# A ring of weight buffers refilled by the half buffer

## The chip, the cores and the metric

The kernel runs on one core of a Trainium2 chip. The metric is the device time of one execution in microseconds (us). It is the median of three runs; a profiled execution beside them gives the trace.

## The reference

One layer of a bidirectional encoder on 512 tokens of width 1024, in float32. Three token mixers (neighbourhood attention, grouped-query attention, attention into 256 memory tokens) are gated and merged, and a layer norm follows. Behind it stands an expert-choice mixture: 16 experts take 64 tokens each.

```python
def expert_choice_ffn(x, w_router, w_gate_up, w_down):
    ...
    gate, idx = lax.top_k(jnp.swapaxes(aff, 1, 2), cap)
    xs = x[bidx, idx]
    h = jnp.einsum('becd,edf->becf', xs, w_gate_up)
    hg, hu = jnp.split(h, 2, axis=-1)
    ye = jnp.einsum('becf,efd->becd', jax.nn.silu(hg) * hu, w_down)
    ye = ye * gate[..., None].astype(ye.dtype)
    return jnp.zeros_like(x).at[bidx, idx].add(ye)
```

The weights of the experts are 16 x (1024 x 2048 + 1024 x 1024) float32 values, 192 MB (of 2^20 bytes). They are read once.

## The kernel before

The program has two stages: the token mixers with the first norm and the routing (up to about 520 us), and the experts with the second norm. Each engine works through its instructions in the order in which they were written. SyncE (SP) issues all transfers of weights, in the order of the program, and an issue that has to wait holds back those behind it.

**Units.** The expert weights are cut into 192 units of 1 MB, [128 partitions x 2048 floats]. A unit `("gu", e, k)` is one of eight parts, along the contraction, of expert e's gate and up matrices; `("dn", e, k)` is one of four parts of its down matrix. `_blocks()` (L44) puts them in the order of use: expert e's first four gate-up units, then the down units of expert e-1, then the rest of expert e's; at the end the gate-up units of expert 15, and the down units of experts 14 and 15.

**The ring.** Twelve places in on-chip memory, listed in `RING` (L32), hold weights in turn; ten have room for two units, `raw` and `VS` for one. The places belong to tiles of the first stage and come free at its end. A *round* is one pass through the list. `ROUNDS` ends the use of `raw` after one round, and of `G1` and `VS` after two. Round one is 12 transfers with 22 units. A *block* is what a place takes in one round: its tag, its width, its units, whether its units are transferred apart (the last `N_SINGLE` units are), and whether the place is used again. In DRAM a block of two units is laid out so that each partition reads 16 KB in one piece.

`Ring.load()` (L807) allocates a new tile at the block's place and issues its transfer at L817, or one per unit at L815 where the units are apart. `Ring.get()` hands out a unit. `Ring.done()` (L835) is called behind the matmuls of a unit, counts down the units that are left in its block, and lends the place on when none is left: the next block is loaded, which waits for the matmuls of both old units.

**The use.** `gate_up(e, ks)` (L1277) does four matmuls for each unit, two for g and two for u (L1285); in the trace each is two instructions, so a unit is 8 records. `down(e)` (L1310) does the same for the down units (L1320), and `last_down` (L1418) for those of expert 15, in quarters of the columns (L1440). While expert 0 runs, steps of a `gather` (L1245, L1247) stand between its units. `combine` adds an expert pair's outputs into the accumulator. In the last expert the residual is prepared ahead, so that behind the last weights little is left: four quarter products, their splits and sums, the statistics of the norm, and eight output transfers (L1547).

Of the kernel before, what the change touches and what calls it, by code (L numbers as in the profile page):

```python
# [18 lines left out]
P = 128  # L19
D = 1024  # L20
# [11 lines left out]
RING = (("Q2", 2), ("Q1", 2), ("Q5", 2), ("Q7", 2), ("Q4", 2), ("Q3", 2), ("Q6", 2), ("raw", 1), ("Q9", 2), ("VS", 1),  # L32
        ("G1", 2), ("M", 2))
ROUNDS = {"raw": 1, "G1": 2, "VS": 2}
N_SINGLE = 10
X_SCALE = 1024.0
A_SCALE = 16384.0

# [1 line left out]
def lead(e):  # L40
    return 2 if e == NEXP - 2 else 4


def _blocks():  # L44
    order = []
    for e in range(NEXP - 1):
        order += [("gu", e, k) for k in range(lead(e))]
        if e:
            order += [("dn", e - 1, k) for k in range(4)]
        order += [("gu", e, k) for k in range(lead(e), KD)]  # L50
    order += [("gu", NEXP - 1, k) for k in range(KD)]
    order += [("dn", e, k) for e in (NEXP - 2, NEXP - 1) for k in range(4)]
    blocks, i, r = [], 0, 0
    while i < len(order):
        for tag, n in RING:
            left = ROUNDS.get(tag, len(order)) - r
            if left > 0 and i < len(order):
                blocks.append((tag, n, order[i:i + n], i + n > len(order) - N_SINGLE, left > 1))
                i += n
        r += 1  # L60
    return blocks

# [2 lines left out]
def layer_kernel(ctx: ExitStack, tc: tile.TileContext, xt, xn, first0, wu, bgate, rpb, gains, wrt,  # L65
                 lnp, lnt, wx, csn, nmask, tri, iota, out, dbg=None):
    nc = tc.nc
# [12 lines left out]
    def R(tag, shape, name, dt=F32, bufs=None):  # L80
        return rp.tile(shape, dt, name=name, tag=tag, bufs=bufs)
# [55 lines left out]
    class Stream:  # L137
        AHEAD_DMA = 2

        def __init__(self):  # L140
            self.nd = 0
            self.ns = 0
            self.used = 0
            self.raw = {}
            self.hl = {}
# [647 lines left out]
    class Ring:  # L793
        def __init__(self):
            self.blocks = _blocks()
            self.at = {}
            self.row = [0]
            for b, (_, n, keys, _, _) in enumerate(self.blocks):
                self.row.append(self.row[-1] + P * n)
                for j, key in enumerate(keys):  # L800
                    self.at[key] = (b, j)
            self.n = 0
            self.left = [len(b[2]) for b in self.blocks]
            self.lent = len(RING)
            self.t = {}
            self.free_at_end = []

        def load(self):
            tag, n, keys, apart, _ = self.blocks[self.n]
            r0 = self.row[self.n]  # L810
            full = R(tag, [P, 2 * n, D], f"w{self.n}")
            src = wx[r0:r0 + P * len(keys)].rearrange("(p j) (h c) -> p (j h) c", j=len(keys), h=2)
            if apart:
                for j in range(len(keys)):
                    nc.sync.dma_start(full[:, 2 * j:2 * j + 2], src[:, 2 * j:2 * j + 2])  # L815
            else:
                nc.sync.dma_start(full[:, :2 * len(keys)], src)  # L817
            for j, key in enumerate(keys):
                t = [full[:, 2 * j + h] for h in range(2)]
                if key[0] == "dn" and key[1] == NEXP - 1:  # L820
                    t = [x.rearrange("p (c n) -> p c n", c=4) for x in t]
                self.t[key] = t
            self.n += 1
# [9 lines left out]
            return self.t.pop(key)  # L833

        def done(self, *key):  # L835
            b, _ = self.at[key]
            self.left[b] -= 1
            if self.left[b] == 0:
                tag, again = self.blocks[b][0], self.blocks[b][4]
                if again:  # L840
                    if self.lent >= len(self.blocks):
                        self.free_at_end.append(tag)
                    self.lent += 1
            self.upto(self.lent)

    ring = Ring()
# [800 lines left out]
def _down_slots(w):  # L1647
    import numpy as np
    a = w.reshape(NEXP, 4, 2, 128, 1024).swapaxes(2, 3).reshape(NEXP, 4, 128, 2048).copy()
    a[-1] = w[-1].reshape(2, 4, 128, 4, 256).transpose(3, 2, 0, 1, 4).reshape(4, 128, 2048)  # L1650
    return a


def _expert_rows(wgu, wdn):
    import numpy as np
    dn = _down_slots(wdn)
    unit = {"gu": lambda e, k: wgu[e, k * P:(k + 1) * P], "dn": lambda e, k: dn[e, k]}
    return np.concatenate([np.stack([unit[t](e, k) for t, e, k in keys], 1).reshape(-1, 2048) for _, _, keys, _, _ in _blocks()])


def _norm_rows(g1, b1, g2, b2):
# [17 lines left out]
def _prep(inp):  # L1679
# [51 lines left out]
    for ty in range(3):  # L1731
# [20 lines left out]
        "lnp": _norm_rows(*(np.asarray(inp[n])[0] for n in ("ln1_g", "ln1_b", "ln2_g", "ln2_b"))),  # L1752
        "lnt": np.stack([np.asarray(inp[n])[0].reshape(8, 128).T for n in ("ln1_g", "ln1_b")], 1),
        "wx": _expert_rows(np.asarray(inp["w_gate_up"])[0], np.asarray(inp["w_down"])[0]),
        "csn": csn, "nmask": nmask, "tri": tri,
        "iota": np.broadcast_to(np.arange(1, 65, dtype=f), (128, 64)),
# [24 lines left out]
```

## Time and profile before

| | |
|---|---|
| runs | 971.08 us median of 3 (971.02 to 971.66) |
| profiled execution, its own time | 973.19 us |
| its span, first to last instruction | 971.3 us |
| granted TensorE clock, mean | 0.996 |
| read from HBM | 247.46 MB |
| DMA queue of SP (q1): packets, MB, share of 16 engines | 37550, 249.74 MB, 63.3% |
| weight transfers | 89 of 2048 KB, 14 of 1024 KB |

The profile gives for each engine the time in which it was busy. PE is the matrix engine, PEld its weight loads, DVE, ACT and POOL are the vector, scalar and GpSimd engines, and SP issues transfers. In the table of stages a row is a stretch of the span: its bounds, its length, then the busy time of each engine with the number of instructions, the granted clock of PE, the mean share of time in which the 16 DMA engines were busy, and the GB/s that they moved. The chain of waits is followed back from the last instruction, at each step to what released it. A matmul that has been issued can count as busy, so a busy PE isn't at its peak by that alone.

### The profile page before, as it was taken

How to read it: one execution, taken by the hardware profiler on the slowest of the kernel's cores; microseconds unless marked ns; L12 is line 12 of the kernel's file. 1: busy time of each engine (PE TensorE's matmuls, PEld its weight loads, DVE VectorE, ACT ScalarE, POOL GpSimd, SP SyncE). 2: the span in 40 equal slices, each digit the busy share in tenths (PEclk: the TensorE clock that was granted, in tenths of full speed). 3: DMA queues.
4: the chain of work that ended last, by engine and by line, in shares of the span. 5: the costliest groups of instructions: out<-in, count | busy, mean ns of one | idle time of the engine just before them, and what ended most of it. 6: DMA issues, size and time to landing. Idle time of an engine off the chain costs nothing.

```text
span 971.3 us, 13273 instructions
## 1 busy us (share of the span) xinstructions
PE 948.8 (98%) x5444; PEld 619.5 (64%) x5444; DVE 454.8 (47%) x866; ACT 276.0 (28%) x544; POOL 79.3 (8%) x86
## 2 busy tenths in 40 slices
PE   9999999999999999999999999999999999998996
PEld 9899878889888888887886333433344333532344
DVE  6347668875376566237464122653322222231426
ACT  5334444544354454323223111100010001100123
POOL 0002303000032231000013000000000000000003
PEclk9999999999999999999999999999999999999998
DMA  9321111211333322575818999999999999999992
GB/s 360 111 68 65 65 66 44 66 46 64 85 112 112 100 82 83 218 285 201 366 61 340 406 431 430 431 430 430 431 431 429 430 431 430 430 429 430 429 396 89
DMA packets 38330, 251.21 MB, mean 259 GB/s; under 512 B 12911, under 2 KB 13295, under 8 KB 24830
## 3 DMA queue, kind: packets, MB, share of 16 engines
q1 hardware_dynamic: 37550, 249.74, 63.3%
q8 instruction: 43, 0.70, 0.3%
q10 hardware_dynamic: 720, 0.62, 0.2%
q14 instruction: 17, 0.14, 0.0%
HBM read 247.46 MB, written 2.10 MB: 257 GB/s over the span
## 4 chain that ended last, share of the span: by engine, by line
PE 80%; DMA 10%; DVE 6%; ACT 1%; issue 1%; POOL 1%; DVEq 0%; POOLq 0%; ACTq 0%; SPq 0%
DMA w<-in_wx 10%; PE g L1285 9%; PE u L1285 9%; PE y L1320 8%; PE gate L274 4%; PE gate L276 4%; PE gate L275 4%; PE pr L274 2%; PE gy L649 2%; PE ga L1245 2%; PE pr L275 2%; PE pr L276 2%; PE nqk L274 1%; PE nqk L275 1%; PE nqk L276 1%; PE gt L636 1%
## 5 line engine op out<-in xcount | busy, mean ns | idle before, releaser
L1285 PE MATMUL g<-w,xs 128*64 128x512 f32 x512 | 135.1, 606 | 3.6 <-DMA w<-in_wx 3.6
L1285 PE MATMUL u<-w,xs 128*64 128x512 f32 x512 | 131.6, 592 | 0.0
L1320 PE MATMUL y<-w,hT 128*64 128x512 f32 x480 | 106.8, 594 | 4.4 <-DMA w<-in_wx 3.7
L93 DVE TENSOR_TENSOR y<-y,y 64x512 fp32r<-64x512 f32 x30 | 20.7, 689 | 134.8 <-ACT y L92 134.8
L1285 PEld LDWEIGHTS u<-w,xs 128*64 128x64 f32 x512 | 36.8, 137 | 73.1 <-issue 72.3
L92 ACT CAST y<-y 64x512 fp32r<-64x512 f32 x30 | 17.4, 579 | 226.1 <-PE y L1320 214.8
L1320 PEld LDWEIGHTS y<-w,hT 128*64 128x64 f32 x480 | 33.7, 137 | 73.8 <-issue 63.2
L93 DVE TENSOR_TENSOR los<-raw_twin,whi 128x1024 fp32r<-128x1024 f32 x43 | 54.1, 1258 | 52.5 <-ACT whi L92 52.3
L276 PE MATMUL gate<-xh,los 128*128 128x512 f32 x192 | 74.8, 390 | 0.0
L1285 PEld LDWEIGHTS g<-w,xs 128*64 128x64 f32 x512 | 30.6, 136 | 55.0 <-issue 43.3
L274 PE MATMUL gate<-xh,whi 128*128 128x512 f32 x160 | 63.5, 397 | 0.0
L275 PE MATMUL gate<-xl,whi 128*128 128x512 f32 x160 | 62.3, 390 | 0.0
L1392 DVE TENSOR_TENSOR acc<-acc,cb 128x512 f32<-128x512 f32 x56 | 35.6, 684 | 37.7 <-PE cb L1390 37.7
L92 ACT CAST whi<-raw_twin 128x1024 fp32r<-128x1024 f32 x43 | 45.1, 1049 | 8.3 <-PE wo L1085 4.4
L93 DVE TENSOR_TENSOR los<-raw_twin,los 128x1024 fp32r<-128x1024 f32 x21 | 26.5, 1260 | 35.5 <-ACT los L92 35.4
L1461 POOL TENSOR_TENSOR acc<-acc,ln2g 128x512 f32<-128x512 f32 x6 | 7.6, 1276 | 432.7 <-DVE l2s L1489 430.7
L276 PEld LDWEIGHTS gate<-xh,los 128*128 128x128 f32 x192 | 36.0, 188 | 7.7
L625 ACT ACTIVATE att_twin<-gs,nm 128x512 f32<-128x512 f32 x32 | 21.7, 683 | 52.4 <-DVE nm L624 52.4
L1295 ACT ACTIVATE tg<-g 128x512 f32<-128x512 f32 x16 | 9.5, 597 | 90.2 <-PE g L1285 90.2
L274 PEld LDWEIGHTS gate<-xh,whi 128*128 128x128 f32 x160 | 30.0, 188 | 7.1 <-issue 1.2
L275 PEld LDWEIGHTS gate<-xl,whi 128*128 128x128 f32 x160 | 30.1, 188 | 5.9
L1308 DVE COPY hT<-ht 128x512 f32<-128x512 f32 x15 | 10.4, 691 | 44.4 <-PE ht L1303 44.4
(420 smaller groups left out, 1902.4 us busy)
## 6 DMA issues: line engine op xcount, KB each, us to landing
w<-in_wx SPq DMA_DIRECT2D x89, 2048.0 KB
raw_twin<-in_wu SPq DMA_DIRECT2D x65, 512.0 KB
w<-in_wx SPq DMA_DIRECT2D x14, 1024.0 KB
raw<-in_wu SPq DMA_DIRECT2D x8, 512.0 KB
xr<-in_xt SPq DMA_DIRECT2D x4, 512.0 KB
macc<-in_xn SPq DMA_DIRECT2D x2, 1024.0 KB
first<-in_first SPq DMA_DIRECT2D x4, 384.0 KB
bf<-in_rpb SPq DMA_DIRECT2D x64, 24.0 KB
```

The costliest lines, as they stand in the source:

```text
L92: nc.scalar.copy(hi, src)
L93: nc.vector.tensor_tensor(lo, src, hi.bitcast(F32), op=ALU.subtract)
L274: nc.tensor.matmul(acc, w_h, rh[:, k], start=(k == 0), stop=False)
L275: nc.tensor.matmul(acc, w_h, rl[:, k], start=False, stop=False)
L276: nc.tensor.matmul(acc, w_l, rh[:, k], start=False, stop=(k == nk - 1))
L625: nc.scalar.activation(self.p[:, h], self.s[h], AF.Exp, bias=nm[:, h:h + 1], accum_out=self.sm[:, h:h + 1])
L649: nc.tensor.matmul(self.y[h * 64:h * 64 + 64, :P], ST["vg"][:, kc, kvh * 64:kvh * 64 + 64], self.pt[:, h, kc], start=(kc == 0), stop=(kc = ...
L1245: nc.tensor.matmul(g, XH[:, m, c], oh[:, m, sl], start=(m == 0), stop=False)
L1285: nc.tensor.matmul(GU[e][b][hf * 64:hf * 64 + 64], xs, w[b][:, hf * 512:hf * 512 + 512], start=(k == 0), stop=(k == KD - 1))
L1308: nc.vector.tensor_copy(t, tp)
L1320: nc.tensor.matmul(y[o * 64:o * 64 + 64], hT[:, c, hf * 64:hf * 64 + 64], w[j][:, o * 512:(o + 1) * 512], start=(k == 0 and j == 0), stop= ...
L1392: nc.vector.tensor_tensor(a, a, cb, op=ALU.add)
```

## The change

The twelve places are allocated once, in round one, and keep their tile (`home`). Round one is as before: whole buffers. From round two on a block is one unit and names the half `h` of its place; its transfer writes that half alone, with 8 KB for each partition, and its DRAM rows are laid out to fit. `done()` lends on after each unit whose place is used again, so the next transfer is issued when the half that it overwrites has been used up. `N_SINGLE` and the split of the last blocks go. For the end, `idle` counts the halves of a place that come free behind the last load; the place is given to `free_at_end` when all of them are.

```diff
-N_SINGLE = 10
...
-                blocks.append((tag, n, order[i:i + n], i + n > len(order) - N_SINGLE, left > 1))
-                i += n
+                for h in range(1 if r == 0 else n):
+                    keys = order[i:i + n] if r == 0 else order[i:i + 1]
+                    if keys:
+                        blocks.append((tag, h, keys, left > 1))
+                        i += len(keys)
...
         def load(self):
-            tag, n, keys, apart, _ = self.blocks[self.n]
-            r0 = self.row[self.n]
-            full = R(tag, [P, 2 * n, D], f"w{self.n}")
-            src = wx[r0:r0 + P * len(keys)].rearrange("(p j) (h c) -> p (j h) c", j=len(keys), h=2)
-            if apart:
-                for j in range(len(keys)):
-                    nc.sync.dma_start(full[:, 2 * j:2 * j + 2], src[:, 2 * j:2 * j + 2])
-            else:
-                nc.sync.dma_start(full[:, :2 * len(keys)], src)
+            tag, h, keys, _ = self.blocks[self.n]
+            src = wx[self.row[self.n]:self.row[self.n + 1]].rearrange("(p j) (h c) -> p (j h) c", j=len(keys), h=2)
+            if tag not in self.home:
+                self.home[tag] = R(tag, [P, 2 * dict(RING)[tag], D], f"w{self.n}")
+            full = self.home[tag][:, 2 * h:2 * h + 2 * len(keys)]
+            nc.sync.dma_start(full, src)
...
         def done(self, *key):
-            b, _ = self.at[key]
-            self.left[b] -= 1
-            if self.left[b] == 0:
-                tag, again = self.blocks[b][0], self.blocks[b][4]
-                if again:
-                    if self.lent >= len(self.blocks):
+            tag, _, _, again = self.blocks[self.at[key]]
+            if again:
+                if self.lent >= len(self.blocks):
+                    self.idle[tag] = self.idle.get(tag, 0) + 1
+                    if self.idle[tag] == dict(RING)[tag]:
                         self.free_at_end.append(tag)
-                    self.lent += 1
+                self.lent += 1
             self.upto(self.lent)
```

More of the change, by code (lines that the diff above doesn't have):

```diff
@@ L797, in __init__ @@
             self.row = [0]
[L798 to L801, printed above, removed]
+            for b, (_, _, keys, _) in enumerate(self.blocks):
+                self.row.append(self.row[-1] + P * len(keys))
+                for key in keys:
+                    self.at[key] = b
             self.n = 0
-            self.left = [len(b[2]) for b in self.blocks]
             self.lent = len(RING)
             self.t = {}
+            self.home = {}
+            self.idle = {}
             self.free_at_end = []
         def load(self):
-            tag, n, keys, apart, _ = self.blocks[self.n]
-            r0 = self.row[self.n]
-            full = R(tag, [P, 2 * n, D], f"w{self.n}")
-            src = wx[r0:r0 + P * len(keys)].rearrange("(p j) (h c) -> p (j h) c", j=len(keys), h=2)
-            if apart:
-                for j in range(len(keys)):
-                    nc.sync.dma_start(full[:, 2 * j:2 * j + 2], src[:, 2 * j:2 * j + 2])
-            else:
-                nc.sync.dma_start(full[:, :2 * len(keys)], src)
+            tag, h, keys, _ = self.blocks[self.n]
[4 more added lines that the diff above has]
+            nc.sync.dma_start(full, src)
             for j, key in enumerate(keys):
-                t = [full[:, 2 * j + h] for h in range(2)]
+                t = [full[:, 2 * j + i] for i in range(2)]
                 if key[0] == "dn" and key[1] == NEXP - 1:
@@ L1657, in _expert_rows @@
     unit = {"gu": lambda e, k: wgu[e, k * P:(k + 1) * P], "dn": lambda e, k: dn[e, k]}
-    return np.concatenate([np.stack([unit[t](e, k) for t, e, k in keys], 1).reshape(-1, 2048) for _, _, keys, _, _ in _blocks()])
+    return np.concatenate([np.stack([unit[t](e, k) for t, e, k in keys], 1).reshape(-1, 2048) for _, _, keys, _ in _blocks()])
 def _norm_rows(g1, b1, g2, b2):
```

## The prediction

> **What bounds the kernel now.** I read the page first, from its head down: span, slices, the chain of waits, the transfers.
>
> ```profile
> span 971.3 us, 13273 instructions
> ...
> DMA  9321111211333322575818999999999999999992
> GB/s 360 111 68 65 65 66 44 66 46 64 85 112 112 100 82 83 218 285 201 366 61 340 406 431 430 431 430 430 431 431 429 430 431 430 430 429 430 429 396 89
> ...
> w<-in_wx SPq DMA_DIRECT2D x89, 2048.0 KB
> ...
> w<-in_wx SPq DMA_DIRECT2D x14, 1024.0 KB
> ```
>
> The slices say that the second half of the span moves about 430 GB/s without a break. That is the expert stage: 89 transfers of 2 MB and 14 of 1 MB, 192 MB of weights. Next come the stages one by one (PE, PEld, DVE, ACT, POOL busy, granted clock, DMA share, GB/s).
>
> ```profile
> 526.00:528.00 2.00, 2.00 (x16) 0.79 (x14) 0.00 (x0) 0.37 (x1) 0.00 (x0) 1.00 0.04 16
> 528.00:545.00 17.00, 17.00 (x108) 6.18 (x104) 3.96 (x12) 2.10 (x6) 0.00 (x0) 1.00 1.00 379
> 526.00:545.00 19.00, 19.00 (x122) 6.97 (x118) 3.96 (x12) 2.47 (x6) 0.00 (x0) 1.00 0.90 341
> 545.00:580.00 35.00, 35.00 (x206) 13.15 (x206) 6.23 (x14) 4.06 (x8) 0.00 (x0) 1.00 1.01 429
> 580.00:880.00 300.00, 299.02 (x1478) 117.30 (x1476) 98.17 (x168) 32.02 (x56) 0.00 (x0) 1.00 1.01 430
> 925.00:940.00 15.00, 13.77 (x64) 4.29 (x62) 3.29 (x8) 2.40 (x4) 0.00 (x0) 1.00 1.01 426
> 922.00:940.00 18.00, 16.77 (x80) 5.59 (x78) 4.15 (x9) 3.70 (x6) 0.00 (x0) 1.00 1.01 425
> 940.00:945.00 5.00, 4.41 (x44) 2.67 (x40) 1.74 (x4) 1.68 (x4) 0.00 (x0) 1.00 0.93 392
> 945.00:950.00 5.00, 4.71 (x67) 4.21 (x68) 2.25 (x7) 0.52 (x2) 0.00 (x0) 1.00 0.18 75
> ```
>
> PE is called busy nearly throughout as well, but from 545 to 940 the DMA share is full, so no earlier request makes that stretch shorter. Ahead of it is a hole of 2 us (16 GB/s) and a ramp of 17 us at 379. The chain of waits (start, length) shows that this stretch sets the end:
>
> ```profile
> 846.93 34.99 DMA w<-in_wx
> 881.98 38.84 DMA w<-in_wx
> 920.83 21.04 DMA w<-in_wx
> 942.01 1.98 PE yq L1440 x32
> ```
>
> Each link is a transfer that SP could issue only when the eighth before it had landed: 846.93 + 34.99 = 881.92 releases the issue at 881.98, and 881.98 + 38.84 = 920.82 that at 920.83. The last link lands at 941.87 and starts the last expert's down product (PE at 942.01). What follows, 971.3 - 942.0 = 29.3 us, is PE, DVE and ACT work on transfers that are of one unit already; only the landing of that one unit moves it. PE's waits (total, times, longest) agree, from 850 on:
>
> ```profile
> PE y L1320 <- DMA w<-in_wx: 3.7, 5, 1.3
> PE g L1285 <- DMA w<-in_wx: 3.6, 5, 1.2
> PE yq L1440 <- DMA w<-in_wx: 0.6, 1, 0.6
> ```
>
> So PE has 3.7 + 3.6 + 0.6 = 7.9 us to spare: the weights may come up to that much earlier and PE follows.
>
> **The change part by part.** Round one (12 transfers, 22 units) stays. The 79 two-unit transfers behind it become 158 of one unit; 12 were single already, so 91 issues become 170. The order of all other work on PE, ACT, DVE and POOL is unchanged, and a read of one half waits only for that half's own transfer.
>
> (a) The hole. First the PE work that frees the first buffer (start, length), then SP's issues: the last of round one and the first of round two.
>
> ```profile
> 522.68 1.08 PE L1285 MATMUL g<-w,xs 128*64 128x512 f32 x4
> 523.59 1.03 PE L1285 MATMUL u<-w,xs 128*64 128x512 f32 x4
> ...
> 525.10 1.08 PE L1285 MATMUL g<-w,xs 128*64 128x512 f32 x4
> 526.01 1.03 PE L1285 MATMUL u<-w,xs 128*64 128x512 f32 x4
> ...
> 519.43 0.33 SPq L817 DMA_DIRECT2D w<-in_wx  x1
> ...
> 527.08 0.33 SPq L817 DMA_DIRECT2D w<-in_wx  x1
> ```
>
> Unit 0 is used up at 523.59 + 1.03 = 524.62, unit 1 at 527.04; the old kernel waits for the second. The new one issues 2.42 us earlier, while round one's last transfer still flows. In the 19 us to 545 the old stream moved what 430 GB/s moves in 19 x 341 / 430 = 15.07 us, so it lost 3.93 us: 2 x (1 - 16/430) = 1.93 in the hole and 17 x (1 - 379/430) = 2.02 in the ramp. The hole goes. The ramp is a stream with hardly a request in hand: PE frees a unit each 525.10 - 522.68 = 2.42 us, and a unit needs 1.0486 MB / 430 = 2.44, so the lead of SP grows slowly here too. Bounds: nothing of the ramp is saved (gain 1.9) or all (3.9). I take half: **-2.9 us**. A larger gain would outrun PE's releases.
>
> (b) The rate. The cost of cutting a transfer in two, both queued, is not shown as such; the one-unit transfers at the end are the nearest row. Bytes: 79 x 2.097 = 165.7 MB, 385.3 us at 430 GB/s. At 426 it is 388.9 (+3.6), at 425 (the window from 922) 389.8 (+4.5). But the landing waits for the last of the 16 DMA engines, and PE's waits show its pace (start, length, idle before):
>
> ```profile
> 932.19 1.94 PE L1320 MATMUL y<-w,hT 128*64 128x512 f32 x8 [0.28 <-DMA w<-in_wx]
> 934.62 1.94 PE L1320 MATMUL y<-w,hT 128*64 128x512 f32 x8 [0.49 <-DMA w<-in_wx]
> ...
> 939.48 1.94 PE L1320 MATMUL y<-w,hT 128*64 128x512 f32 x8 [0.46 <-DMA w<-in_wx]
> ```
>
> Three units in 7.29 us, 2.43 each; by the chain two-unit transfers take 38.90 / 8 = 4.86, the same per unit: +0. Between 0 and +4.5 I take **+1.3 us**, a third of the mean price, nearer to the row of the engine that sets the landing. The eight links to 941.87 took 21.05 us for 8 units, 1.6 more than the pace; were that a price of halves it would be 1.6 x 158 / 8 = 32 us, but the later waits at 2.43 and the mean of 425 exclude it: it is one step.
>
> The Trainium skill speaks against this part: "DMA: Bandwidth & Descriptors", section "Anatomy of one DMA", gives each transfer a fixed 2 us beside its bytes. By that the sum would be 79 x 2 = 158 us worse. The rows at 425 and 426 GB/s, transfers of 1 MB behind one another, don't show it: that cost lies under the queue.
>
> (c) The laggard. After 940 the rate falls to 392 and 75 instead of ending at once: the engines are some us apart, and the last counts. Part of this may come from the hole and ramp. Bounds 0 and -2 us; I take **-0.6**.
>
> (d) What is queued. SP carries nothing else until the outputs at the end, so its waits on the eighth transfer before delay only weights. Eight halves hold 8 x 2.44 = 19.5 us of flow. The longest stop of PE's releases that I found lies between SP's issues
>
> ```profile
> 609.90 0.33 SPq L817 DMA_DIRECT2D w<-in_wx  x1
> ...
> 620.76 0.33 SPq L817 DMA_DIRECT2D w<-in_wx  x1
> ```
>
> 10.9 us, under the 19.5, so the queue doesn't run dry; if it did, each such stop would cost the excess. 79 more issues at 0.33 us are 26 us of SP, in its idle time. PE gets 79 waits more; at 0.1 us each, were they not free, the 7.9 us would just cover them.
>
> **Sum:** -2.9 + 1.3 - 0.6 = **-2.2 us**. The profiled execution took 973.19 us, 1.9 around its span of 971.3; the median of the three runs is 971.08, 2.1 below it. The stages behind each term don't differ for that, so the change is taken from the median: 971.08 - 2.2 = **968.9 us**.
>
> **The rivals.** *It cancels.* The ramp stays whole, because a request that comes 2.4 us ahead is still late (-1.9), the rate costs its bound from the end row, halved (+1.8), and the laggard stays: 971.0 us. For it: PE's 2.42 against 2.44 us per unit, which lets no lead build up. Against: the 2 us hole certainly goes.
>
> *The small transfer costs throughput: slower.* All engines run the 158 halves at the 425 GB/s of the row from 922: +4.5, the hole alone is won, -1.9, together +2.6: 973.7 us. For it: two windows of halves both lie below 430. Against: PE's waits at 2.43. It passes the gain of 3.5 (a and c) where two halves take 3.5 / 79 = 44 ns more than a whole, and gives a loss that can be told from 69 ns on.
>
> *Every transfer pays a start of its own:* each of the 79 added ones would lose what the hole before round two costs, 1.93 us, 152 us in all: 1123 us. The rows at 425 and 426 GB/s speak against it, unless halves queue differently in mid-stream. Chance 0.01. This is the Trainium skill's fixed cost (the section named under b) taken bare.
>
> *The halves don't part:* a read would wait for the refill of the other half. Each expert would then lose a landing, at least one 2.44 us per unit, over 300 us. The new program's waits don't hold this. Chance 0.01.
>
> **How the numbers follow.** Three runs spread by 0.07%, so a change within 0.2% (1.9 us) can't be told from none. The forecast, gain over 1.9 us: 0.47. It cancels: 0.34. Throughput rival: 0.17. The last two: 0.02 together. Range: the best ends give -3.9 + 0 - 2 = -5.9, hardly all at once; the worst +2.6. I cut the near side at -4.4 and end the far one at +2.3: 966.7 to 973.4, both signs in it; the forecast's own range is 966.7 to 969.1. Faster 0.47, same 0.34, slower 0.19.
>
> **What would show it.** The first issue of round two at about 524.7 instead of 527.1; the window 526 to 528 near 400 GB/s, and 528 to 545 over 400. The windows from 580 to 880 at 428 to 429; at 426 or less the throughput rival has it. In the chain the landing ahead of the last down product near 939.7 instead of 941.9, with the 29.3 us behind it unchanged. PE waiting on weights from 850 on, for some 5 to 8 us, and not before. I am wrong if the stream shows a hole at 610 to 620, if PE waits for weights before 850, or if the 29.3 us at the end change.

## The result, and the profile after

| | before | after |
|---|---|---|
| median of 22 runs each, us | 970.63 (968.86 to 971.66) | 972.11 (971.26 to 972.71) |
| ratio, with its 95% interval | 1 | 1.0016 (1.0010 to 1.0023) |
| profiled execution, its own time, us | 973.19 | 972.15 |
| its span, us | 971.3 | 970.4 |

The 22 runs of before include the three shown ahead. The changed kernel is slower by 0.16%, 0.0016 x 970.63 = 1.6 us. The interval lies wholly above 1; the forecast had been 2.2 us faster.

The two spans point the other way, and that has to be cleared first. It comes from that one execution of before, in which PE's clock fell about 400 us ahead of the experts. This is the table of stages for one stretch, before and then after; the third number from the end is the granted clock of PE.

```profile
123.00:127.00 4.00, 4.00 (x13) 3.33 (x14) 1.78 (x3) 1.16 (x2) 0.00 (x0) 0.57 0.28 109
```

```profile
123.00:127.00 4.00, 4.00 (x19) 3.27 (x19) 2.67 (x5) 1.17 (x2) 0.00 (x0) 1.00 0.14 58
```

The clock fell to 0.57 of full speed over these 4 us in the profiled execution of before, in none of the other eleven, and expert 0 begins at 522.68 there and at 520.50 in after. So the stages are compared from the first matmul of expert 0 on, and the first experiment below gives a second profile of before's transfers.

The page of after:

```profile
span 970.4 us, 13445 instructions
...
GB/s 360 113 67 66 66 66 44 67 66 45 113 105 94 97 82 87 243 282 210 332 88 355 424 426 427 427 427 426 427 426 427 427 427 427 427 427 428 426 399 88
...
q1 hardware_dynamic: 48926, 249.74, 64.1%
...
w<-in_wx SPq DMA_DIRECT2D x172, 1024.0 KB
w<-in_wx SPq DMA_DIRECT2D x10, 2048.0 KB
```

The steady slices stand at 426 to 427 GB/s, where before had 429 to 431, and the queue takes 48926 - 37550 = 11376 packets more for the same 249.74 MB: 79 x (128 + 16), 128 pieces and 16 small packets for each added transfer. The table of stages splits the stretch that the weights set: the first 24 us from expert 0's first matmul, and the 380 us behind them. First before, then after; the last number of a row is GB/s.

```profile
522.68:546.68 24.00, 24.00 (x152) 9.04 (x154) 5.12 (x17) 3.37 (x8) 0.00 (x0) 1.00 0.92 356
546.68:926.68 380.00, 373.21 (x1852) 143.39 (x1848) 118.95 (x204) 41.77 (x74) 0.00 (x0) 1.00 1.01 430
```

```profile
520.50:544.50 24.00, 24.00 (x152) 9.04 (x154) 5.12 (x17) 3.37 (x8) 0.00 (x0) 1.00 0.97 387
544.50:924.50 380.00, 373.85 (x1852) 143.21 (x1848) 118.98 (x204) 41.81 (x74) 0.00 (x0) 1.00 1.01 427
...
524.00:526.00 2.00, 2.00 (x17) 0.79 (x14) 0.00 (x0) 0.46 (x1) 0.00 (x0) 1.00 0.95 369
526.00:529.00 3.00, 3.00 (x20) 1.08 (x18) 0.41 (x1) 0.00 (x0) 0.00 (x0) 1.00 0.83 281
526.00:543.00 17.00, 17.00 (x106) 6.04 (x102) 3.96 (x12) 2.02 (x5) 0.00 (x0) 1.00 0.96 381
...
610.00:620.00 10.00, 10.00 (x84) 6.99 (x81) 5.98 (x16) 2.26 (x4) 0.00 (x0) 1.00 1.00 423
```

Two terms stand here. The start gains 24 x (387 - 356) / 430 = 1.7 us. The steady stream runs at 427 instead of 430 GB/s. Rates rounded to 1 GB/s are coarse for this loss, but the view of the transfers also counts the packets that begin in the same 380 us, and their MB. First before, then after; "under 512 B" are the small packets, 16 for each transfer.

```profile
DMA packets 11538, 163.44 MB, mean 430 GB/s; under 512 B 1280, under 2 KB 1280, under 8 KB 1280
```

```profile
DMA packets 22241, 162.09 MB, mean 427 GB/s; under 512 B 2471, under 2 KB 2471, under 8 KB 2471
```

The steady stream loses 380 x (163.44 - 162.09) / 162.09 = 3.2 us. The whole refills and the second copy of after, both described below, moved 163.39 and 162.07 MB in their 380 us, which gives 3.1, the number used from here on. The chain of waits of after (start, length) agrees:

```profile
838.49 19.62 DMA w<-in_wx
858.18 19.50 DMA w<-in_wx
877.74 20.79 DMA w<-in_wx
898.59 19.55 DMA w<-in_wx
...
920.63 19.55 DMA w<-in_wx
940.31 1.98 PE yq L1439 x32
```

A link is eight transfers of one unit. From landing to landing it is 19.57 us in the second row and 19.61 in the fourth, 2.45 us per unit, against 38.90 / 16 = 2.43 in the chain of before. That is some 0.02 us per half, times 158 = 3 us. The link of 20.79 is of this execution alone, as the 21.04 of before is.

The third term lies behind the last landing. From the last down product to the end of the span it is 970.4 - 940.31 = 30.1 us, where before had 29.3: 0.8 us more. Added up, -1.7 + 3.1 + 0.8 = +2.2 us; the timed runs say +1.6, with an interval from 1.0 to 2.2.

### The profile page after: what moved, and what is told of

Read it like the earlier page. It is cut to its first block, busy times and chain, and to the rows that moved or that the text cites. A ratio compares the mean times of both kernels' runs of the same rounds, so it can differ in the third digit from the quotient of the medians.

```text
span 970.4 us, 13445 instructions
## 1 busy us (share of the span) xinstructions
PE 947.5 (98%) x5444; PEld 617.5 (64%) x5444; DVE 454.8 (47%) x866; ACT 276.4 (28%) x544; POOL 81.2 (8%) x86
## 3 DMA queue, kind: packets, MB, share of 16 engines
q1 hardware_dynamic: 48926, 249.74, 64.1%
## 4 chain that ended last, share of the span: by engine, by line
PE 65%; DMA 24%; DVE 6%; ACT 1%; issue 1%; POOL 1%; DVEq 0%; POOLq 0%; SPq 0%; ACTq 0%
DMA w<-in_wx 24%; PE g L1284 6%; PE u L1284 5%; PE gate L276 4%; PE y L1319 4%; PE gate L277 4%; PE gate L278 4%; PE pr L276 2%; PE gy L651 2%; PE pr L277 2%; PE pr L278 2%; PE nqk L276 2%; PE nqk L278 1%; PE nqk L277 1%; PE gt L638 1%
## 5 line engine op out<-in xcount | busy, mean ns | idle before, releaser
L277 PEld LDWEIGHTS gate<-xl,whi 128*128 128x128 f32 x160 | 30.1, 188 | 5.9
```

The costliest lines, as they stand in the source:

```text
L277: nc.tensor.matmul(acc, w_h, rl[:, k], start=False, stop=False)
```

## The experiments

Each compares itself with runs of before that were taken beside it on the same chip. "Stretch" is the time from expert 0's first matmul to the first down product of expert 15 (L1440 of before), both read from the timeline of PE; "end" is from there to the end of the span.

| kernel | ratio (95% interval) | first 24 us, next 380 us, GB/s | stretch, us | end, us |
|---|---|---|---|---|
| before | 1 | 356, 430 | 419.3 | 29.3 |
| whole refills again | 1.0004 (0.9995 to 1.0012) | 356, 430 | 418.1 | 29.3 |
| after | 1.0016 (1.0010 to 1.0023) | 387, 427 | 419.8 | 30.1 |
| second copy of after | 1.0019 (1.0011 to 1.0028) | 386, 427 | 419.6 | 30.0 |
| whole, 8 KB pieces | 1.0029 (1.0018 to 1.0041) | 360, 427 | 421.1 | 29.2 |
| whole, 4 KB pieces | 1.0085 (1.0070 to 1.0101) | 348, 421 | 427.4 | 29.3 |
| halves, late | 1.0039 (1.0027 to 1.0051) | 358, 427 | 422.1 | 29.4 |
| halves in round two | 0.9990 (0.9981 to 0.9999) | 389, 430 | 416.5 | 29.7 |
| 4 halves | 1.0001 (0.9990 to 1.0011) | 368, 430 | 417.3 | 29.3 |
| 14 halves | 0.9991 (0.9982 to 1.0000) | 384, 430 | 416.7 | 29.4 |
| 14 halves, again | 0.9983 (0.9974 to 0.9992) | 391, 430 | 416.7 | 29.4 |
| after, fetch moved | 1.0018 (1.0010 to 1.0027) | 392, 426 | 419.4 | 29.4 |

### Whole refills of buffers that keep their place

The ring is written so that each block states which units must be used up before it loads (`after`), and `MODE` says how a block is cut. Here the buffers are laid out once, as in the change, but refilled whole.

```diff
+def MODE(r, i, total):
+    return "apart" if i + 2 > total - 10 else "whole"
...
+                cut = MODE(r, i - n, len(order))
+                if r == 0 or cut == "whole":
+                    blocks.append((tag, 0, keys, left > 1, tuple(keys)))
+                else:
+                    for h, key in enumerate(keys):
+                        blocks.append((tag, h, [key], left > 1, tuple(keys) if cut == "apart" else (key,)))
...
-            full = R(tag, [P, 2 * n, D], f"w{self.n}")
+            if tag not in self.home:
+                self.home[tag] = R(tag, [P, 2 * dict(RING)[tag], D], f"w{self.n}")
+            full = self.home[tag][:, 2 * h:2 * h + 2 * len(keys)]
...
+            while self.n < len(self.blocks) and self.used.issuperset(self.after[self.n]):
+                self.load()
```

> Buffers allocated once, but refilled whole (two units in one transfer) when both units are used up, the last ten units apart, as before the change. Everyone expects no difference from before: allocation alone moves no instruction. The stretch from expert 0's first matmul to expert 15's first down product is 419.3 us in the trace of before; here 419.3 +- 0.7, and 430 GB/s between 580 and 880 us. If allocation once were itself the cost (waits across the whole buffer), this kernel would be 1.5 us slower, as the changed one is.

Measured 970.47 us, ratio 1.0004. Laying the buffers out once costs nothing that these runs can tell. Its table of stages and its chain are a second profile of before's transfers:

```profile
520.14:544.14 24.00, 24.00 (x152) 9.04 (x154) 5.12 (x17) 3.37 (x8) 0.00 (x0) 1.00 0.91 356
544.14:924.14 380.00, 373.00 (x1850) 143.39 (x1848) 118.95 (x204) 41.81 (x74) 0.00 (x0) 1.00 1.01 430
...
524.00:526.00 2.00, 2.00 (x18) 0.90 (x16) 0.00 (x0) 0.46 (x1) 0.00 (x0) 1.00 0.43 98
526.00:543.00 17.00, 17.00 (x111) 6.21 (x108) 3.96 (x12) 2.02 (x5) 0.00 (x0) 1.00 0.97 382
```

```profile
879.65 38.83 DMA w<-in_wx
918.54 19.56 DMA w<-in_wx
```

Both rates repeat, 356 and 430, and so does the link of 38.83. But the last link, the same eight one-unit transfers that took 21.04 us in before's chain, takes 19.56 here. The step of 1.5 us in before was of that one execution, and it explains why before's stretch in the table is 1.2 us longer than this one's, where 419.3 +- 0.7 had been expected.

### One-unit transfers, meant to be issued late

This cut and those that follow are against the kernel of whole refills, where nothing else is said.

```diff
 def MODE(r, i, total):
-    return "apart" if i + 2 > total - 10 else "whole"
+    return "apart"
```

> Transfers of one unit from round two on, but both halves are issued only when both units are used up: the small transfer without the early issue. Theory of the two terms: the hole of 2 us and the ramp stay, the stream runs at 427 instead of 430 GB/s, so 2.5 to 3.5 us slower than before, and 1 to 2 us slower than the changed kernel. Rival, that the small transfer costs nothing and the changed kernel's loss lies in its end or elsewhere: within 0.7 us of before.

The edit missed its aim. The list `after` orders the program, but the transfer waits on the chip only for the reads of the bytes that it overwrites, and these are those of its own half. SP's first issue of round two shows it:

```profile
522.24 0.33 SPq L831 DMA_DIRECT2D w<-in_wx  x1
```

Expert 0 begins at 520.26, so the issue comes 1.98 us behind it, as in after (522.48 - 520.50 = 1.98). What ran is a second copy of the change, and as such it is of use: 971.92 us, 1.0019, with 386 and 427 GB/s.

### Whole transfers in shorter pieces

A transfer of two units reads 16 KB in one piece for each partition. Here its units lie one behind the other in DRAM, so the same 2 MB transfer, issued at the same time, is made of 8 KB pieces, as the halves are.

```diff
-            src = rows.rearrange("(p j) (h c) -> p (j h) c", j=len(keys), h=2)
-            nc.sync.dma_start(full, src)
+            src = rows.rearrange("(j p) n -> p j n", j=len(keys))
+            nc.sync.dma_start(full.rearrange("p (j h) c -> p j (h c)", h=2), src)
```

> Whole-buffer refills of 2 MB as before, but each unit lies by itself in DRAM, so that a partition reads two pieces of 8 KB instead of one of 16 KB. If the price of the changed kernel's stream is the length of the piece, the rate is 427 GB/s here too and the time 2.5 to 3.5 us above before. If it is the number of transfers, the rate stays at 430 and the time within 0.7 us of before.

Later the same was done with 4 KB:

```diff
+    wx2 = wx.rearrange("r (h c) -> (r h) c", h=2)
...
+            rows = wx2[2 * self.row[self.n]:2 * self.row[self.n + 1]]
+            src = rows.rearrange("(j h p) n -> p (j h) n", j=len(keys), h=2)
```

> Whole-buffer refills of 2 MB as before, in pieces of 4 KB (four for each partition). If each piece costs a fixed few nanoseconds beside its bytes, as 2 x 309 ns for 8 KB against 611 ns for 16 KB and 159 ns for the 4 KB pieces of the first stage say, the rate falls further, to about 420 GB/s between 580 and 880 us, and the time is 8 to 11 us above before. If 8 KB pieces were slow for another reason (two places in DRAM for each partition), 4 KB need not be slower than those: 426 GB/s, 3 us above before.

Stages and transfers of the 380 us in the 8 KB kernel, then in the 4 KB kernel:

```profile
544.42:924.42 380.00, 372.06 (x1836) 142.51 (x1832) 117.01 (x202) 40.19 (x71) 0.00 (x0) 1.00 1.01 427
...
DMA packets 21056, 162.29 MB, mean 427 GB/s; under 512 B 1260, under 2 KB 1260, under 8 KB 1260
```

```profile
544.66:924.66 380.00, 366.32 (x1810) 139.94 (x1808) 114.59 (x198) 38.82 (x69) 0.00 (x0) 1.00 1.02 421
...
DMA packets 40203, 159.86 MB, mean 421 GB/s; under 512 B 1221, under 2 KB 1221, under 8 KB 40186
```

Measured 972.98 us (1.0029) and 979.04 us (1.0085). With no more transfers than before, 8 KB pieces give the 427 GB/s of after, and 4 KB pieces 421. So most of the rate term is the price of the shorter piece: 380 x (163.44 - 162.29) / 162.29 = 2.7 us of the 3.1. The remaining half a microsecond goes with the number of transfers, 162.29 MB here against 162.09 in after. The price of a piece is nearly the same at both lengths. Pieces are the packets without the small ones, 11538 - 1280 = 10258 in before and 21056 - 1260 = 19796 here: 2.7 us x 16 engines / (19796 - 10258) = 4.5 ns. For 4 KB it is 380 x (163.44 - 159.86) / 159.86 = 8.5 us, and with 40203 - 1221 = 38982 pieces 8.5 x 16 / (38982 - 10258) = 4.7 ns.

### Halves, late

This is the experiment that the second copy had been meant to be, made in another way. The cut is against the kernel before, with its own switch for units apart set in every later round. Each round allocates a new tile, so both halves wait for the whole buffer.

```diff
-                blocks.append((tag, n, order[i:i + n], i + n > len(order) - N_SINGLE, left > 1))
+                blocks.append((tag, n, order[i:i + n], r > 0 and len(order[i:i + n]) > 1 or i + n > len(order) - N_SINGLE, left > 1))
```

> The kernel before with each buffer of round two and later filled by two transfers of one unit, but both waiting until the whole buffer is used up: small transfers without the early issue. The theory: the start loses its 4.3 us as before, the stream 3.4 us more than with two-unit transfers, the end 0.7 us by SP's fetch, so 3.5 to 4.5 us above before and 2 us above the changed kernel. Rival, that the early issue gained nothing: the same as the changed kernel, 1.5 us above before.

The stages, and SP's first issues:

```profile
520.12:544.12 24.00, 24.00 (x152) 9.04 (x154) 5.13 (x17) 3.37 (x8) 0.00 (x0) 1.00 0.90 358
544.12:924.12 380.00, 372.72 (x1844) 142.23 (x1840) 117.77 (x203) 41.32 (x74) 0.00 (x0) 1.00 1.01 427
```

```profile
524.52 0.80 SPq L815 DMA_DIRECT2D w<-in_wx  x2
```

The first issue stands 4.40 us behind expert 0's begin, as in before, the start is before's (358), the rate is after's (427): 973.55 us, 1.0039. Against after, the same transfers issued late cost 0.0039 - 0.0016 = 0.0023, 2.2 us, and 422.1 - 419.8 = 2.3 us of the stretch; the windows say 24 x (387 - 358) / 427 = 1.6. So the early issue is worth some 2 us, and cutting the transfers costs more than that. The 162.07 MB of its 380 us are after's too. The time is in the expected range, but not by the expected sum: no 0.7 us came at the end, which stays at 29.4.

### Halves only where the lead is short

If the gain is made at the start and the loss everywhere, the halves belong to the start alone. Three lengths were tried: round two (21 units), 4 units, and 14 units; the last ten units are apart as in before.

```diff
+    return "half" if r == 1 else "apart" if i + 2 > total - 10 else "whole"
...
+    return "half" if r == 1 and i < 26 else "apart" if i + 2 > total - 10 else "whole"
...
+    return "half" if r == 1 and i < 36 else "apart" if i + 2 > total - 10 else "whole"
```

> Half-buffer refills in round two alone (21 units), two-unit transfers from round three on, the last ten units apart. Theory of the two terms: the early issue's gain of about 2 us is kept, the small transfers cost 10 pairs x 0.04 = 0.4 us, so 1 to 2 us faster than before and 2.5 to 3.5 us faster than the changed kernel. Rival, that the gain at the start is given back later (PE's releases pace the stream, or the end doesn't hang on the stream): within 0.7 us of before.

> Half-buffer refills for the first two buffers of round two alone (4 units), two-unit transfers behind them. If the ramp comes from SP's small lead over the stream, a lead that is short again after four units costs part of the gain: the stream's landings come 0.5 to 1.2 us earlier than with whole refills, not 2, and the time is 0.4 to 1.2 us under before. If the early first issue alone makes the gain, it is as large as with a whole round of halves: 2 us earlier landings, 1.5 to 2 us under before.

> Half-buffer refills for the first seven buffers of round two (14 units), two-unit transfers behind them, the last ten units apart. The theory: the start gains 2 us, the 7 cut transfers cost 0.3 us, and SP's stream is short enough that no fetch falls at the end (6.8 to 7.0 us from the last matmul), so 1.3 to 2 us under before, and 0.3 to 1 us under halves for the whole of round two. Rival, that the lead is lost again at the change to two-unit transfers: within 0.7 us of before.

> The kernel with half-buffer refills for 14 units of round two once more, for the interval. Expected 0.7 to 1.5 us under before, as the first time, with 7.0 us from the last matmul to the end. Rival, that the first time was chance: not under before.

Stages of the kernel with 21 halves, with 4, and with 14 (its second run):

```profile
520.52:544.52 24.00, 24.00 (x152) 9.03 (x154) 5.12 (x17) 3.37 (x8) 0.00 (x0) 1.00 0.98 389
544.52:924.52 380.00, 374.58 (x1858) 144.44 (x1856) 119.04 (x204) 41.81 (x74) 0.00 (x0) 1.00 1.01 430
```

```profile
520.21:544.21 24.00, 24.00 (x152) 9.03 (x154) 5.12 (x17) 3.37 (x8) 0.00 (x0) 1.00 0.97 368
...
524.00:526.00 2.00, 2.00 (x18) 0.82 (x16) 0.00 (x0) 0.46 (x1) 0.00 (x0) 1.00 0.92 365
526.00:543.00 17.00, 17.00 (x110) 6.21 (x107) 3.96 (x12) 2.01 (x5) 0.00 (x0) 1.00 0.96 359
```

```profile
521.14:545.14 24.00, 24.00 (x152) 9.03 (x154) 5.11 (x17) 3.37 (x8) 0.00 (x0) 1.00 0.98 391
545.14:925.14 380.00, 374.20 (x1855) 144.14 (x1852) 118.90 (x204) 41.81 (x74) 0.00 (x0) 1.00 1.01 430
```

With 21 halves the start of after (389) comes with the rate of before (430): 969.31 us, 0.9990. With 14 it is 968.95 us (0.9991) and 969.01 (0.9983, interval 0.9974 to 0.9992): faster than before by about 0.1 to 0.2%, and than after by some 0.25 to 0.33%. By the interval of its second run this version beats both kernels. The gains of the first two runs are at or under the low end of what was expected (some 1.0 us for 21 halves, 0.9 for 14). Four halves do not gain: 970.28 us, 1.0001. They fill the hole (365 GB/s against 98 in the whole refills) and lose over half of it again behind (359 against 382): 2 x (365 - 98) / 430 = 1.2 us gained, 17 x (382 - 359) / 430 = 0.9 lost. Over the 24 us 0.7 us are left (368 against 356), and the trace's stretch is 0.8 us shorter; the runs, 0.9990 to 1.0011, don't confirm a gain. The first whole transfer behind the halves again waits for two units. That little is in the queue then, and that 14 halves keep the gain because the queue holds more, is a reading that fits these rows; what the queue held was not measured.

### The end

After's 0.8 us at the end had no term in the forecast. The transfers of the last 12 us (GB/s in forty slices of 0.3 us, then the queue that carries instructions: packets, MB, share) of after, and the slices of the whole refills:

```profile
GB/s 0 0 0 0 0 0 0 0 0 0 321 389 417 416 383 410 396 396 396 437 403 376 410 410 410 383 423 205 27 14 0 0 0 0 0 0 0 0 0 0
...
q14 instruction: 1, 0.01, 0.2%
```

```profile
GB/s 0 0 0 287 410 410 389 410 423 396 403 410 417 382 410 423 417 382 410 423 191 0 0 0 0 0 0 0 0 0 0 0 0 0 0 0 0 0 0 0
```

The outputs of after do not stop at once: two slices of 27 and 14 GB/s trail, 0.6 us in which, by the packets of the trace, the last seven output packets of 2 KB go one behind another, as from one engine. In the same window stands one transfer of instructions, which the whole refills do not have there. The second copy has both too, with 34 and 27 trailing. The late halves have as many transfers of weights as after, but no transfer of instructions among the last outputs, and their end is 29.4 us; so the longer end doesn't come from one-unit transfers as such. The theory is that more instructions on SP move the point at which a block of its program is fetched in among the last outputs; whose instructions they are, the trace doesn't say. To move it on, after was given twelve tiny transfers more in mid-stream; they bring 256 bytes each into a tile that nothing reads.

```diff
         def load(self):
             tag, h, keys, _ = self.blocks[self.n]
+            if 60 <= self.n < 156 and self.n % 8 == 4:
+                k = (self.n - 60) // 8
+                nc.sync.dma_start(pad[:, 4 * k:4 * k + 4], iota[:16, :4])
```

> The changed kernel with 12 more transfers of SP, 256 bytes each into a tile of their own, spread over the expert stage. They move the place in SP's instruction stream where its next piece of instructions is fetched. Theory: in the changed kernel that fetch (965.9 us in its trace) falls among the last waits for the outputs and costs some 0.7 us there; here it falls earlier, so the time from the last matmul to the end of the span is 6.8 to 7.0 us, as before the change, not 7.7, and the whole is 0.3 to 0.7 us under the changed kernel (12 small transfers cost up to 0.4 us). Rival, that the longer end comes from the ring of halves itself: the end stays at 7.7 us.

```profile
GB/s 0 0 0 0 0 0 0 177 416 410 396 396 423 416 376 423 410 410 383 423 423 376 410 416 307 0 0 0 0 0 0 0 0 0 0 0 0 0 0 0
```

The transfer of instructions is gone from the window, the trail too, and the end is 29.4 us instead of 30.1. The kernel with 21 halves has a transfer of instructions of 8 KB too, 1.4 us behind its last output packet, and an end of 29.7; the other eight traces, without one there, have 29.2 to 29.4. In the traces the theory holds, for the place and the size. In the runs it could not be confirmed: 971.64 us, 1.0018 (1.0010 to 1.0027) against 1.0016 for after. The profiled execution is the fastest of its eleven (970.72), so its short end need not be the usual one. The added transfers may also have cost what the end won, or the two ratios are too wide to tell 0.7 us; that is open.

## Why the prediction was wrong

Forecast was 2.2 us faster; measured is 1.6 us slower, a miss of 3.8. The early issue worked as foreseen. What failed above all is step (b), the price of the rate, with step (a), the ramp, behind it: -1.7 + 3.1 in place of -2.9 + 1.3 turns the sum from -2.2 to +0.8. The term (c) brought nothing and the end had no term. All four misses are to the same side.

**(a) The start, -2.9: it is -1.7.** The early issue came as foreseen, 1.98 us behind the begin of expert 0, and the hole is filled: 369 GB/s where before has 16 and the whole refills 98. But I had half of the ramp saved as well, and in this trace nothing of it was: 381 GB/s in the 17 us behind, against 379 in before and 382 in the whole refills. The other kernels with 14 halves or more have 383 to 396 there, at most 0.6 us above the whole refills. SP's issues show that hardly a lead builds up:

```profile
522.48 0.33 SPq L817 DMA_DIRECT2D w<-in_wx  x1
...
524.90 0.33 SPq L817 DMA_DIRECT2D w<-in_wx  x1
...
527.32 0.33 SPq L817 DMA_DIRECT2D w<-in_wx  x1
```

They come 2.42 us apart, one for each unit that PE frees, and the stream dips to 281 at 526 to 529 instead of stopping ahead of it. The lower bound of the term, the hole alone at -1.9, was near the number. What exactly a transfer needs in hand to run at the full rate was not measured; four halves are too few and 14 are enough.

**(b) The rate, +1.3: it is +3.1.** This is the largest miss, 1.8 us. I had the right rows, 425 and 426 GB/s in the windows of one-unit transfers, worth +3.6 to +4.5, and set them aside for three waits of PE at 2.43 us per unit. The difference is 0.02 us per unit, and three waits can't show it. In after the same kind of row reads (start, length, idle before):

```profile
930.41 1.94 PE L1319 MATMUL y<-w,hT 128*64 128x512 f32 x8 [0.47 <-DMA w<-in_wx]
932.86 1.94 PE L1319 MATMUL y<-w,hT 128*64 128x512 f32 x8 [0.52 <-DMA w<-in_wx]
...
937.81 1.94 PE L1319 MATMUL y<-w,hT 128*64 128x512 f32 x8 [0.51 <-DMA w<-in_wx]
```

2.45 us for the first unit, 2.475 each for the next two: the spread between neighbours is as large as the price. A window of hundreds of us, or a chain of many transfers, was the row to use. The mechanism was off as well: I had priced the cut into two transfers, but 2.7 of the 3.1 us come from the shorter pieces.

The Trainium skill has the rule for it, which the prediction passed over: "DMA: Bandwidth & Descriptors", section "Why small descriptors are slow (HBM only)", gives each packet about 3 cycles beside its bytes, and the section "Where 436 GB/s comes from" a fabric of 850 MHz, so an estimate by the page is 3 / 0.85 = 3.5 ns a piece. The runs show 4.5 and 4.7 ns, the same size and about a third more, at pieces far longer than the 256 bytes that the page reckons with. The rule that the prediction did weigh, a fixed 2 us per transfer, stands in the same page for the path by way of GpSimd, while SP issues these transfers; it would be 158 us, where the added transfers cost about 0.5 us here.

**(c) The laggard, -0.6: nothing.** The last link was 21.04 us in before, 19.56 in the whole refills and 19.55 in after. The 1.6 us above the pace were indeed one step and no price of halves, as the prediction says, but a step of that execution, which this change does not win back. The stream itself ran at 426 GB/s through that link of before, so what came late was the landing and not the flow. The fall at the end that the term was read from stays too: in the 5 us from 2 us ahead of the last expert's first down product the rate is 418 GB/s in the whole refills and in after, and in the next 5 us it is 149 and 118.

**(d) What is queued: right.** 423 GB/s from 610 to 620, so the stream shows no hole there. PE's list of waits from 519 to 850 has none for weights. Over the whole run it has (total, times, longest):

```profile
PE y L1319 <- DMA w<-in_wx: 4.7, 7, 1.7
PE g L1284 <- DMA w<-in_wx: 2.1, 5, 0.5
...
PE yq L1439 <- DMA w<-in_wx: 0.6, 1, 0.6
```

7.4 us, within the 5 to 8 foreseen; 79 issues and waits more cost SP and PE nothing to be seen.

**The end, unchanged: +0.8.** That it might change was named among the signs of an error, but it had no term. I had counted SP's added issues as idle time. If the theory of the fetch holds, what was left out is the bringing in of their instructions.

**The rivals.** "The small transfer costs throughput" is nearest: it has the sign, the start at -1.9 and +2.6 in all, with 4.5 for a rate term of 3.1 and without the end. "It cancels" has the same start, but its +1.8 for the rate is 1.3 short, and the end is missing. The other two are out: no hole follows each transfer, and the halves part, or the first issue would not stand behind the first unit.

## What to carry to other kernels

A transfer that is split so that it can start earlier gained here only where the stream ran dry, and paid in every piece; split the transfers at that place, more than the first few (here 4 units were too few and 14 enough), and keep the long pieces in the steady stream. Price a difference of a per cent in the rate from a window of hundreds of us or a chain of many transfers, never from a few waits. Where a kernel ends in a short serial tail, look whether a fetch of instructions falls among the last outputs; two traces here have one.

## What the runs showed of the hardware

- The rate of queued reads falls with the piece length at one size of transfer: 430 GB/s at 16 KB for each partition, 427 at 8 KB, 421 at 4 KB, about 4.5 ns for each added piece on its engine. Twice as many transfers at the same piece length cost some 0.5 us in 380 (162.29 against 162.09 MB).
- A transfer of instructions (queue q14) among the last outputs goes with 0.6 us in which the outputs trail at 14 to 34 GB/s.
- A link of the chain is now and then 0.6 to 1.5 us above its pace (21.04 in before, 20.79 in after, 20.21 in the late halves). The windows of these three links each hold a transfer of the other queue of instructions (q8), but so do links that keep the pace (19.56 in the whole refills), so this cause is not settled. The stream does not slow in them: 426, 428 and 426 GB/s.
- PE's granted clock can be near half for some us in one profiled execution of twelve: 0.57 over 4 us, and expert 0 began 2.2 us later than in after.
